# A two-layer hybrid encoder on one core: 512-column matmuls over high and low activations in the gate and up projections

## The chip, the cores and the metric

The kernel runs on one core of one Trainium2 chip. The time is the device time of one execution in microseconds, the median of several runs. A profile is one execution of the same program, recorded instruction by instruction. The engines in it are PE (the matmul engine, whose weight loads are listed as PEld), DVE (the vector engine), ACT (the scalar engine) and SP, which here only issues DMAs. POOL does nothing in this kernel.

## The reference

A sequence of 256 tokens of width 1024 goes through two layers. Each layer is a gated feed-forward sub-layer at half weight, a token-mixing sub-layer (retention, stick-breaking attention and a state-space mixer side by side) and a second feed-forward sub-layer. All is float32. Cut to what matters here:

```python
def swiglu(u, wg, wu, wd):
    return (jax.nn.silu(u @ wg) * (u @ wu)) @ wd

for l in range(DEPTH):                       # DEPTH = 2
    mod = (cond @ ada_w[l] + ada_b[l])       # shift, scale and gate of the sub-layers
    u = modulate(rmsnorm(h, norm_ffn1[l]), mod[0], mod[1])
    h = h + 0.5 * (1.0 + mod[2]) * swiglu(u, ffn1_wg[l], ffn1_wu[l], ffn1_wd[l])
    ...                                      # token mixing
    u = modulate(rmsnorm(h, norm_ffn2[l]), mod[6], mod[7])
    h = h + 0.5 * (1.0 + mod[8]) * swiglu(u, ffn2_wg[l], ffn2_wu[l], ffn2_wd[l])
```

The width of the feed-forward layer is 2816, which is 11 blocks of 256 columns.

## The kernel before

**Products in three parts.** PE multiplies in a rounded float32 form (`fp32r`). To keep float32 accuracy the kernel splits every weight and every activation into a high part, rounded to that form, and a low part, the rest. A product is then three matmuls that add up in one place of PSUM: high weights times high activations, high weights times low activations, low weights times high activations (`mm3`). Each matmul has 128 x 128 weights and 256 columns, the 256 tokens. Each matmul instruction has its own weight load in the profile, also where two in a row use the same weights.

**Units.** The weights come as units of 1 MB: one gate block (g), one up block (u) or one down block (d) of 256 columns or rows. A unit has two halves. For each half ACT copies the raw weights into the high part (`hi`, L306) and DVE subtracts to get the low part (`lo`, L307). There are eight buffers each for `hi` and `lo`. `half` and `need` see to it that, when PE's code comes to a half, the splits of the seven halves behind it have been issued ahead of it. A split whose buffer is still in use waits for PE. The order in which units are fetched and split is a fixed list (`SEQ`). Between the weight units it also holds 80 units of the modulation weights `ada_w`, two DVE instructions each (`raw_a`, L266); where they fall is set by the table `ADA_SPANS`. They are densest in the two feed-forward sub-layers of the first layer.

**A feed-forward sub-layer** (`ffn`) goes through the blocks j. For each j PE runs the gate projection into one PSUM bank (`pg`), then the up projection into another (`pu`), and then a down unit of an earlier block (`dn`). ACT takes the silu straight from `pg` (L195, called in `ffn`), DVE multiplies by `pu` straight from PSUM (L611), and `gated` splits the product into high and low (ACT and DVE, 512 columns each). The down unit of block j runs only after the gate and up units of block j+1. All engines take their instructions in the order in which the code issues them.

**PSUM.** There are eight banks of 512 float32 columns. A ring of four one-bank tiles serves `pg`, `pu`, the lead and the mixing sub-layer; four more banks hold the output sums (`dn`).

**The lead.** In all sub-layers but the first, the first gate and up units (four blocks of 128 columns, f = 0 to 3) run on activations that are not yet normalised (`hgh`, `hgl`), so that PE works while the norm is computed (`lead`). They go into four banks `ld`, 258 columns each. At the end, for each f, PE finishes the last two of eight steps, ACT reads one column (`lbias`), and DVE scales the rest (`lt`, L483). Between these, DVE and ACT make the normalised activations (`nt`, `uh`, `ul`). The next two units run interleaved step by step (`proj2`), since the activations only just become ready. The first sub-layer uses `start` for its first three blocks instead.

**Counts.** 76 gate and up units run outside leads and start: 8 blocks in the first feed-forward sub-layer and 10 in each of the other three, two units each. A unit has 8 steps over the width and 2 column blocks, so 16 products of three matmuls: 1216 in all.

Of the kernel before, what the change touches and what calls it, by code (L numbers as in the profile page):

```python
# [155 lines left out]
class Trunk:  # L156
# [5 lines left out]
    def __init__(self, ctx, tc, io):  # L162
        self.tc, self.nc, self.io = tc, tc.nc, io
        pool = lambda name, bufs, **kw: ctx.enter_context(tc.tile_pool(name=name, bufs=bufs, **kw))
        self.cp = pool("const", 1)
        self.rawp = pool("raw", self.NRAW)
        self.hip = pool("whi", self.NHALF)
        self.lop = pool("wlo", self.NHALF)
        self.t2 = pool("t2", 5)
        self.sm = pool("small", 2)  # L170
        self.ring = pool("ringp", 4, space=PSUM)
        self.pool = pool
        self.early = tc.tile_pool(name="early", bufs=self.NEARLY)
        self.earlyp = self.early.__enter__()
        self.raw = {}
        self.w = {}
        self.sent = 0
        self.done = 0
        self.ready = -1
        self.procs = []  # L180
        self.table = None
# [18 lines left out]
    def mm3(self, out, w, u, start, flip=False):  # L200
        for n, (a, b) in enumerate(((0, 0), (0, 1), (1, 0))):
            x, y = (u[b], w[a]) if flip else (w[a], u[b])
            self.mm(out, x, y, start and n == 0)

    def bank(self, name):
        return self.ring.tile([P, 512], F32, tag="ring", name=name)

    def open_acc(self, pairs):
        self.accs = self.tc.tile_pool(name="accp", bufs=2 if pairs else 4, space=PSUM)
# [99 lines left out]
    def setup(self):  # L309
        nc, io = self.nc, self.io  # L310
        self.params = self.cp.tile([P, NPAR], F32, name="params")
        self.consts = self.cp.tile([P, NCST], F32, name="consts")
        self.cond = self.cp.tile([P, 1024], F32, name="cond")
        self.wdt = self.cp.tile([P, L, 8, 8], F32, name="wdt")
        self.mods = self.cp.tile([P, NA * 2], F32, name="mods")
        self.h = self.cp.tile([P, KD, S], F32, name="h")
        self.uh = self.cp.tile([P, KD, S], FR, name="uh")
        self.ul = self.cp.tile([P, KD, S], FR, name="ul")
        self.rs = self.cp.tile([P, S], F32, name="rs")
        self.mats = self.cp.tile([P, 4, P], FR, name="mats")  # L320
        self.eps = self.cp.tile([P, 1], F32, name="eps")
        nc.vector.memset(self.eps, EPS)
        nc.sync.dma_start(out=self.cond, in_=io["c"].broadcast_to([P, 1024]))
        nc.sync.dma_start(out=self.params, in_=io["params"])
        for _ in range(self.NRAW + self.NEARLY + 1):
            self.send()
        self.silu(out=self.cond, in_=self.cond)
# [121 lines left out]
        self.nc.vector.scalar_tensor_tensor(out=self.ul[:, c], in0=t, scalar=self.mods[:, self.shift + c:self.shift + c + 1],  # L449
                                            in1=self.uh[:, c].bitcast(F32), op0=ALU.add, op1=ALU.subtract)  # L450

    def lead(self, n, ends):
        nc = self.nc
        banks = [self.bank("ld") for _ in range(4)]

        def go(k, f):
            hf = k // 4
            hi, lo = self.w[n + f // 2, hf]
            cs = slice((f % 2) * P, (f % 2) * P + P)
            gh, gl = self.hg[hf]  # L460
            self.mm3(banks[f][:, 0:258], [hi[:, k % 4, cs], lo[:, k % 4, cs]], (gh[:, k % 4], gl[:, k % 4]), k == 0)

        self.need(n + 1, 1, 2)
        for k in range(6):
            if k == 5:
                self.norm_sum(self.acc("nps"))
                self.need(n + 1, 1, 3)
                self.norm_rstd()
                self.need(n + 1, 1, 4)
            for f in range(4):  # L470
                go(k, f)
        self.norm_bcast()
        bias = self.sm.tile([P, 4], F32, tag="lbias", name="lbias")
        ts, us = [], []
        for f in range(4):
            for k in (6, 7):
                go(k, f)
            nc.scalar.activation(out=bias[:, f:f + 1], in_=banks[f][:, 256:257], func=AF.Copy)
            us.append(self.apply_a(f))
            if f % 2 == 0:  # L480
                t = self.tk2("lt")
            ts.append(t[:, (f % 2) * 256:(f % 2) * 256 + 256])
            nc.vector.tensor_tensor(out=ts[f], in0=banks[f][:, 0:256], in1=self.rs, op=ALU.mult)  # L483
# [55 lines left out]
    def proj_k(self, bank, w, k, flip, banks):  # L539
        w = [t[:, k % 4] for t in w]  # L540
        for f in range(2):
            if flip:
                self.mm3(banks[f], w, [t[:, f * P:(f + 1) * P] for t in self.u(k)], k == 0, True)
            else:
                cs = slice(f * P, (f + 1) * P)
                self.mm3(bank[:, f * 256:(f + 1) * 256], [t[:, cs] for t in w], self.u(k), k == 0 and f == 0)

    def proj(self, bank, n, flip=False, banks=None):
# [14 lines left out]

    def ffn(self, w0, gate_col, prep, start=None):
        nc = self.nc
        self.open_acc(False)
        n = w0 + 2
        pend = []

        def gated(sg):  # L570
            g = self.tk4("g", FR)
            gh, gl = (g[:, 2 * i:2 * i + 2] for i in range(2))
            flat = lambda t: t.rearrange("p a b -> p (a b)")
            self.split(flat(gh), flat(gl), sg)
            pend.append([(gh[:, f], gl[:, f]) for f in range(2)])

        def ends(f, t, b):
            v = sg[:, (f % 2) * 256:(f % 2) * 256 + 256]
            if f < 2:
                self.silu(out=v, in_=t, bias=b)  # L580
            else:
                nc.vector.scalar_tensor_tensor(out=v, in0=t, scalar=b, in1=v, op0=ALU.add, op1=ALU.mult)

        g0 = 1
        if start:
            g0 = GS
            banks = start()
            n = w0 + 2 * GS
            self.need(n, 0, 2)
            for j in range(GS):  # L590
# [3 lines left out]
                gated(sg)  # L594
        else:
            sg = self.tk2("sg")
            self.lead(w0, ends)
            gated(sg)
        accs = None
        for j in range(g0, NJ):  # L600
            pg, pu = self.bank("pg"), self.bank("pu")
            pair = j == 1
            if pair:
                self.proj2(n, (pg, False, None), (pu, False, None))
            else:
                self.proj(pg, n)
            sg = self.tk2("sg")
            self.silu(out=sg, in_=pg)
            if not pair:
                self.proj(pu, n + 1)  # L610
            nc.vector.tensor_tensor(out=sg, in0=sg, in1=pu, op=ALU.mult)  # L611
# [12 lines left out]
        self.out_unit(accs, n, pend.pop(0), False, True, gate)  # L624
        self.close_acc()

    def mix(self, l, w0, gate_col, prep):
        nc = self.nc
        st = {}
        flat = lambda t: t.rearrange("p a b -> p (a b)")  # L630
        V = lambda t, n: flat(t).rearrange("p (a b) -> p a b", a=n)
        self.open_acc(True)
        dt = self.sm.tile([P, 2, 8], F32, tag="dt", name="dt")
        dta = self.sm.tile([P, 2, 8], F32, tag="dta", name="dta")
# [316 lines left out]
        for o, kk in enumerate(W_OUT_ORDER):  # L951
# [5 lines left out]
            self.out_unit(accs, n, mov, o == 0, o == 5, gate)  # L957
            n += 1
        self.close_acc()

    def run(self):
        nc = self.nc
# [8 lines left out]
        for l in range(L):  # L971
            m, n = l * 72, l * NSUB
            self.ffn(n, m + 16, prep, None if l else lambda: self.start(*first))
            self.mix(l, n + NF, m + 40, prep)
            self.ffn(n + NF + NM, m + 64, prep)
        mean = self.bank("mean")[:, 0:256]
        for n, sq in enumerate(self.sq):
            for f in range(2):
# [9 lines left out]
        for b, o in enumerate(out):  # L988
            for f in range(2):
# [3 lines left out]
                else:  # L993
                    nc.scalar.activation(out=o[:, f], in_=o[:, f], func=AF.Identity, bias=sh)
            nc.sync.dma_start(out=self.io["out"][:, 2 * b:2 * b + 2], in_=o)


def _pack(inp):
# [96 lines left out]
```

## Time and profile before

| | |
|---|---|
| device time, median of 3 runs | 1162.9 us (1162.77 to 1163.27) |
| span of the profiled execution, first to last instruction | 1161.9 us |
| feed-forward sub-layers in the span, about | 27 to 219, 409 to 599, 599 to 789, 970 to 1150 us |
| mixing sub-layers, about | 219 to 409, 789 to 970 us |
| granted PE clock | 0.998 |
| weights and other data read | 280 MB |

The profiled execution's own device time is not listed apart from its span. The median of the runs is 1.0 us above the span: what lies around the first and the last instruction.

In a group's row stand line, engine, operation, names (out <- in), shapes and count, then the busy time of the group in us, the mean ns of one instruction, and the idle time of its engine just ahead of them with what ended it. In a timeline row stand the start in us, the duration, engine, line, names and shapes; idle time ahead of the row is in brackets. Matmuls overlap: one of 256 columns is listed with 280 ns, while the next starts 0.12 us after it, so what one costs is the distance of the starts. `f32` in a row of PE stands for both float32 forms.

### The profile page before, as it was taken

Reading aid. Unit: us, or ns where it says so; the run is one execution under the profiler, and the core shown is the slowest. Engines: PE = TensorE matmul, PEld = TensorE weight load, DVE = VectorE, ACT = ScalarE, POOL = GpSimd, SP = SyncE. Lnnn points to the kernel's source line nnn. Section 1 sums busy time; section 2 is a strip of 40 time slices with the busy share of each in tenths; the row PEclk is TensorE's granted clock in tenths of the full one; section 3 lists DMA queues with packets and bytes.
Section 4 is the critical chain, followed back from the end, with each engine's and each line's share of the span. In section 5 each row is a group of like instructions: output and inputs, shape, how many; then the busy total and the mean of one; then the engine's idle time right before and its main releaser. Section 6 shows DMA issues by size and latency. Waiting matters only on the chain.

```text
span 1161.9 us, 22045 instructions
## 1 busy us (share of the span) xinstructions
PE 1126.8 (97%) x9316; PEld 1115.7 (96%) x9316; DVE 893.3 (77%) x1300; ACT 619.0 (53%) x870; POOL 0.2 (0%) x4
## 2 busy tenths in 40 slices
PE   1999999999999999999999999999999999999996
PEld 1999999999999999999999999999999999999996
DVE  6988786788778788898488788667886877977544
ACT  4464434586874464444466444457687546544432
POOL 0000000000000000000000000000000000000000
PEclk9999999999999999999999999999999999999999
DMA  9879898357454539999536988643655452987610
GB/s 376 338 265 366 320 361 333 129 214 276 163 190 155 182 142 370 347 372 359 188 110 258 345 322 307 254 182 144 256 182 186 177 189 80 351 331 283 235 58 37
DMA packets 39555, 282.63 MB, mean 243 GB/s; under 512 B 4384, under 2 KB 4640, under 8 KB 5408
## 3 DMA queue, kind: packets, MB, share of 16 engines
q1 hardware_dynamic: 39456, 281.22, 64.6%
q8 instruction: 73, 1.20, 0.4%
q14 instruction: 26, 0.21, 0.1%
HBM read 280.15 MB, written 1.05 MB: 242 GB/s over the span
## 4 chain that ended last, share of the span: by engine, by line
PE 96%; DVE 2%; ACT 1%; DMA 1%; issue 0%; SPq 0%; ACTq 0%; DVEq 0%
PE dn L198 21%; PE pu L198 19%; PE pg L198 19%; PE pj L198 14%; PE ld L198 7%; PE wo L198 6%; PE pv L198 4%; DVE raw_a L266 1%; PE seg L198 1%; PE nps L198 1%; DMA h<-in_x 1%; PE tail L198 1%; PE sz L198 1%; PE rn L198 1%; PE yb L198 1%; PE rs L198 0%
## 5 line engine op out<-in xcount | busy, mean ns | idle before, releaser
L307 DVE TENSOR_TENSOR lo<-raw_w,hi 128x1024 fp32r<-128x1024 f32 x368 | 441.6, 1222 | 152.8 <-ACT hi L306 152.5
L306 ACT ACTIVATE hi<-raw_w 128x1024 fp32r<-128x1024 f32 x368 | 380.3, 1053 | 252.4 <-DMA raw_w<-in_w 118.1
L198 PE MATMUL dn<-g,hi 128*128 128x256 f32 x1408 | 250.7, 280 | 0.0
L198 PEld LDWEIGHTS dn<-g,hi 128*128 128x128 f32 x1408 | 215.7, 189 | 0.0
L266 DVE CUSTOM_DVE_ANT_0 raw_a<-raw_a,cond,params 128x1024 f32<-128x1024 f32 x160 | 198.8, 1280 | 0.3 <-DMA raw_a<-in_ada 0.3
L198 PE MATMUL dn<-g,lo 128*128 128x256 f32 x704 | 197.3, 280 | 0.0
L198 PE MATMUL pu<-uh,hi 128*128 128x256 f32 x608 | 171.2, 282 | 0.0
L198 PE MATMUL pu<-ul,hi 128*128 128x256 f32 x608 | 171.2, 282 | 0.0
L198 PE MATMUL pg<-ul,hi 128*128 128x256 f32 x608 | 171.1, 281 | 0.0
L198 PE MATMUL pg<-uh,hi 128*128 128x256 f32 x608 | 171.1, 281 | 0.0
L198 PE MATMUL pg<-uh,lo 128*128 128x256 f32 x608 | 170.9, 281 | 0.0
L198 PE MATMUL pu<-uh,lo 128*128 128x256 f32 x608 | 170.8, 281 | 0.0
L198 PEld LDWEIGHTS dn<-g,lo 128*128 128x128 f32 x704 | 132.8, 189 | 0.0
L198 PE MATMUL pj<-uh,hi 128*128 128x256 f32 x448 | 127.9, 285 | 0.0
L198 PE MATMUL pj<-ul,hi 128*128 128x256 f32 x448 | 126.0, 281 | 0.0
L198 PE MATMUL pj<-uh,lo 128*128 128x256 f32 x448 | 125.9, 281 | 0.0
L198 PEld LDWEIGHTS pu<-uh,lo 128*128 128x128 f32 x608 | 114.9, 189 | 0.0
L198 PEld LDWEIGHTS pg<-uh,lo 128*128 128x128 f32 x608 | 114.8, 189 | 0.0
L198 PEld LDWEIGHTS pu<-ul,hi 128*128 128x128 f32 x608 | 114.5, 188 | 0.0
L198 PEld LDWEIGHTS pg<-ul,hi 128*128 128x128 f32 x608 | 114.4, 188 | 0.0
L198 PEld LDWEIGHTS pg<-uh,hi 128*128 128x128 f32 x608 | 114.4, 188 | 0.0
L198 PEld LDWEIGHTS pu<-uh,hi 128*128 128x128 f32 x608 | 114.3, 188 | 0.0
(189 smaller groups left out, 1791.2 us busy)
## 6 DMA issues: line engine op xcount, KB each, us to landing
raw_w<-in_w SPq DMA_DIRECT2D x184, 1024.0 KB, 5.8
raw_a<-in_ada SPq DMA_DIRECT2D x80, 1024.0 KB, 6.5
consts<-in_consts SPq DMA_DIRECT2D x1, 1216.0 KB, 10.1
h<-in_x SPq DMA_DIRECT2D x1, 1024.0 KB, 7.0
out<-fin SPq DMA_DIRECT2D x4, 256.0 KB, 2.3
cond<-in_c SPq DMA_DIRECT2D x1, 512.0 KB, 4.3
mats<-in_mats SPq DMA_DIRECT2D x1, 256.0 KB, 7.1
params<-in_params SPq DMA_DIRECT2D x1, 176.0 KB, 4.4
```

The source lines that it names most:

```text
L198: self.nc.tensor.matmul(out, lhsT=lhsT, rhs=rhs, start=start, stop=True, skip_group_check=True)
L266: nc.vector.tensor_tensor_reduce(out=raw[:, f * 1024:(f + 1) * 1024], in0=raw[:, f * 1024:(f + 1) * 1024], in1=self.cond, scale=1.0, scala ...
L306: self.nc.scalar.activation(out=hi, in_=src, func=AF.Copy)
L307: self.nc.vector.tensor_tensor(out=lo, in0=src, in1=hi.bitcast(F32), op=ALU.subtract)
```

## The change

High and low activations now lie side by side in one tile (`us`). For the 76 gate and up units, one matmul takes the high weights against both, 512 columns, into a full bank: columns 0 to 255 get the high part, 256 to 511 the low part. A second matmul of 256 columns adds low weights times high activations onto the first half. A block of 256 weight columns thus needs two banks (`bank2`), and the ring has two such tiles in place of four of one bank. The sum of the two halves is made at reading (`fold`): ACT copies the low half from PSUM into SBUF, DVE adds the high half from PSUM. The silu then works on SBUF, and the up projection is folded too before the multiplication. The leads of the three later feed-forward sub-layers take their four banks as two of the two-bank tiles. The ring is opened and closed in each sub-layer. Leads, down units, the mixing sub-layer and the order of the weights keep their matmuls.

```diff
+    def lead_banks(self, pairs):
+        if pairs:
+            return [t[:, f] for t in [self.bank2("ld") for _ in range(2)] for f in range(2)]
+        return [self.bank("ld") for _ in range(4)]
...
+    def wide_k(self, bank, w, k):
+        hi, lo = (t[:, k % 4] for t in w)
+        both = self.us[:, k].rearrange("p a b -> p (a b)")
+        for f in range(2):
+            cs = slice(f * P, (f + 1) * P)
+            self.mm(bank[:, f], hi[:, cs], both, k == 0)
+            self.mm(bank[:, f, 0:256], lo[:, cs], self.uh[:, k], False)
...
+    def wide2(self, n, names):
+        banks = [self.bank2(name) for name in names]
+        for k in range(KD):
+            if k % 4 == 0:
+                wa = self.half(n, k // 4, 1)
+                wb = self.half(n + 1, k // 4, 3)
+            self.wide_k(banks[0], wa, k)
+            self.wide_k(banks[1], wb, k)
+        return banks
+
+    def fold(self, bank, name):
+        t = self.tk2(name)
+        v = t.rearrange("p (a b) -> p a b", a=2)
+        self.nc.scalar.activation(out=v, in_=bank[:, :, 256:512], func=AF.Copy)
+        self.nc.vector.tensor_tensor(out=v, in0=v, in1=bank[:, :, 0:256], op=ALU.add)
+        return t
...
         for j in range(g0, NJ):
-            pg, pu = self.bank("pg"), self.bank("pu")
             pair = j == 1
             if pair:
-                self.proj2(n, (pg, False, None), (pu, False, None))
+                pg, pu = self.wide2(n, ("pg", "pu"))
             else:
-                self.proj(pg, n)
-            sg = self.tk2("sg")
-            self.silu(out=sg, in_=pg)
+                pg = self.wide("pg", n)
+            sg = self.fold(pg, "sg")
+            self.silu(out=sg, in_=sg)
             if not pair:
-                self.proj(pu, n + 1)
-            nc.vector.tensor_tensor(out=sg, in0=sg, in1=pu, op=ALU.mult)
+                pu = self.wide("pu", n + 1)
+            t = self.fold(pu, "su")
+            nc.vector.tensor_tensor(out=sg, in0=sg, in1=t, op=ALU.mult)
             gated(sg)
```

What moves in the instruction order is shown at three places. Names carry buffer numbers; `lo68_0` is the low part of the first half of unit 68, and a wait names the engine whose semaphore is waited for. In the second feed-forward sub-layer of the first layer unit 67 is the gate unit of block 3, 68 its up unit, 69 the down unit behind them.

DVE, in the order before, around the up unit of block 2 (`raw_a` is the modulation work):

```order
L307 TENSOR_TENSOR lo68_0_4936<-raw_w68_4422,hi68_0_4935 128x1024 [waits DMAHW5_49,PE_49,Activation_49]
L307 TENSOR_TENSOR lo68_1_4966<-raw_w68_4422,hi68_1_4965 128x1024 [waits PE_49,Activation_49]
L266 ISA raw_a35_4601,mods_85<-raw_a35_4601,cond_83,params_81 128x1024 [waits DMAHW6_49,DVE_49]
...
L307 TENSOR_TENSOR lo69_0_5000<-raw_w69_4749,hi69_0_4999 128x1024 [waits DMAHW7_49,PE_49,Activation_49]
L611 TENSOR_TENSOR sg_4963<-sg_4963,pu_4900 128x512 [waits PE_49]
L307 TENSOR_TENSOR g_5028<-sg_4963,g_5028 128x512 [waits Activation_49]
L307 TENSOR_TENSOR lo69_1_5032<-raw_w69_4749,hi69_1_5031 128x1024 [waits Activation_49]
```

DVE, the same place in the changed kernel:

```order
L321 TENSOR_TENSOR lo68_0_4697<-raw_w68_4217,hi68_0_4696 128x1024 [waits DMAHW5_49,PE_49,Activation_49]
L592 TENSOR_TENSOR sg_4716<-sg_4716,pg_4669 128x512 [waits Activation_49]
L321 TENSOR_TENSOR lo68_1_4722<-raw_w68_4217,hi68_1_4721 128x1024 [waits Activation_49]
L280 ISA raw_a35_4398,mods_82<-raw_a35_4398,cond_80,params_78 128x1024 [waits DMAHW6_49,DVE_49]
...
L321 TENSOR_TENSOR lo69_0_4748<-raw_w69_4530,hi69_0_4747 128x1024 [waits DMAHW7_49,PE_49,Activation_49]
L592 TENSOR_TENSOR su_4767<-su_4767,pu_4720 128x512 [waits Activation_49]
L663 TENSOR_TENSOR sg_4716<-sg_4716,su_4767 128x512 [waits DVE_49]
L321 TENSOR_TENSOR g_4771<-sg_4716,g_4771 128x512 [waits Activation_49]
L321 TENSOR_TENSOR lo69_1_4775<-raw_w69_4530,hi69_1_4774 128x1024 [waits Activation_49]
```

Two adds (L592) have come in: that of `pg` between the two splits of unit 68, that of `pu` ahead of the multiplication.

ACT at the same place, before:

```order
L306 ACTIVATE hi68_0_4935<-raw_w68_4422 128x1024 [waits DMAHW5_49,PE_49,Activation_49]
L195 ACTIVATE sg_4963<-pg_4899 128x512 [waits PE_49]
L306 ACTIVATE hi68_1_4965<-raw_w68_4422 128x1024 [waits DVE_49]
L306 ACTIVATE hi69_0_4999<-raw_w69_4749 128x1024 [waits DMAHW7_49,DVE_49,PE_49]
L306 ACTIVATE g_5028<-sg_4963 128x512 [waits DVE_49]
```

ACT, changed:

```order
L320 ACTIVATE hi68_0_4696<-raw_w68_4217 128x1024 [waits DMAHW5_49,PE_49,Activation_49]
L591 ACTIVATE sg_4716<-pg_4669 128x512 [waits PE_49]
L194 ACTIVATE sg_4716<-sg_4716 128x512 [waits DVE_49]
L320 ACTIVATE hi68_1_4721<-raw_w68_4217 128x1024 [waits Activation_49]
L320 ACTIVATE hi69_0_4747<-raw_w69_4530 128x1024 [waits DMAHW7_49,PE_49,Activation_49]
L591 ACTIVATE su_4767<-pu_4720 128x512 [waits PE_49]
L320 ACTIVATE g_4771<-sg_4716 128x512 [waits DVE_49]
```

The silu (L194) now stands behind a wait for DVE, and the split of `hi68_1` stands behind the silu.

PE at the end of the lead of the same sub-layer, changed: the last step of block f = 1 and of f = 3, and the first matmuls of the next two units.

```order
L197 MATMUL ld_4311<-hgh_4207,lo59_1_4118 128x258
L197 MATMUL ld_4311<-hgh_4207,hi59_1_4117 128x258 [waits DVE_49]
...
L197 MATMUL ld_4312<-hgh_4207,hi60_1_4145 128x258 [waits DVE_49]
...
L197 MATMUL pg_4488<-us_84,hi61_0_4175 128x512 [waits PE_49]
L197 MATMUL pg_4488<-us_84,lo61_0_4176 128x256
...
L197 MATMUL pu_4489<-us_84,hi62_0_4213 128x512 [waits DVE_49]
```

PE, before, from the last matmul of the lead on:

```order
L198 MATMUL ld_4515<-hgh_4412,lo60_1_4351 128x258
L198 MATMUL pg_4691<-uh_87,hi61_0_4380 128x256 [waits DVE_49,Activation_49]
L198 MATMUL pg_4691<-ul_88,hi61_0_4380 128x256 [waits DVE_49]
L198 MATMUL pg_4691<-uh_87,lo61_0_4381 128x256
...
L198 MATMUL pu_4692<-uh_87,hi62_0_4418 128x256 [waits Activation_49]
```

Blocks f = 0 and 1 now share one tile `ld`, and f = 2 and 3 another. The end of f = 1 waits for DVE's reading of f = 0, that of f = 3 for the reading of f = 2, and the first matmul of `pu` for the reading of f = 3; before, none of these waits was there. In steady state the first matmul of each `pg` and `pu` now waits for DVE, whose add has freed the tile.

More of the change, by code (lines that the diff above doesn't have):

```diff
@@ L170, in __init__ @@
         self.sm = pool("small", 2)
-        self.ring = pool("ringp", 4, space=PSUM)
         self.pool = pool
@@ L203, in mm3, with open_ring, close_ring, bank2 @@
             self.mm(out, x, y, start and n == 0)
+    def open_ring(self, pairs):
+        self.rings = self.tc.tile_pool(name="ringp", bufs=2 if pairs else 4, space=PSUM)
+        self.ring = self.rings.__enter__()
+    def close_ring(self):
+        self.rings.__exit__(None, None, None)
     def bank(self, name):
         return self.ring.tile([P, 512], F32, tag="ring", name=name)
+    def bank2(self, name):
+        return self.ring.tile([P, 2, 512], F32, tag="ring", name=name)
+    def lead_banks(self, pairs):
+        if pairs:
+            return [t[:, f] for t in [self.bank2("ld") for _ in range(2)] for f in range(2)]
+        return [self.bank("ld") for _ in range(4)]
     def open_acc(self, pairs):
@@ L316, in setup @@
         self.h = self.cp.tile([P, KD, S], F32, name="h")
-        self.uh = self.cp.tile([P, KD, S], FR, name="uh")
-        self.ul = self.cp.tile([P, KD, S], FR, name="ul")
+        self.us = self.cp.tile([P, KD, 2, S], FR, name="us")
+        self.uh, self.ul = self.us[:, :, 0], self.us[:, :, 1]
         self.rs = self.cp.tile([P, S], F32, name="rs")
@@ L450, in apply_b, with lead @@
                                             in1=self.uh[:, c].bitcast(F32), op0=ALU.add, op1=ALU.subtract)
-    def lead(self, n, ends):
+    def lead(self, n, ends, pairs=False):
         nc = self.nc
-        banks = [self.bank("ld") for _ in range(4)]
+        banks = self.lead_banks(pairs)
         def go(k, f):
@@ L546, in proj_k, with wide @@
                 self.mm3(bank[:, f * 256:(f + 1) * 256], [t[:, cs] for t in w], self.u(k), k == 0 and f == 0)
+    def wide_k(self, bank, w, k):
[5 more added lines that the diff above has]
+            self.mm(bank[:, f, 0:256], lo[:, cs], self.uh[:, k], False)
+    def wide(self, name, n):
+        bank = self.bank2(name)
+        for k in range(KD):
+            if k % 4 == 0:
+                w = self.half(n, k // 4)
+            self.wide_k(bank, w, k)
+        return bank
+    def wide2(self, n, names):
+        banks = [self.bank2(name) for name in names]
+        for k in range(KD):
+            if k % 4 == 0:
+                wa = self.half(n, k // 4, 1)
[9 more added lines that the diff above has]
+        return t
     def proj(self, bank, n, flip=False, banks=None):
@@ L565, in ffn @@
         nc = self.nc
+        self.open_ring(not start)
         self.open_acc(False)
@@ L594, in ffn @@
                 gated(sg)
+            self.close_acc()
+            self.close_ring()
+            self.open_ring(True)
+            self.open_acc(False)
         else:
             sg = self.tk2("sg")
-            self.lead(w0, ends)
+            self.lead(w0, ends, True)
             gated(sg)
@@ L625, in ffn @@
         self.close_acc()
+        self.close_ring()
     def mix(self, l, w0, gate_col, prep):
@@ L631, in mix @@
         V = lambda t, n: flat(t).rearrange("p (a b) -> p a b", a=n)
+        self.open_ring(False)
         self.open_acc(True)
@@ L959, in mix @@
         self.close_acc()
+        self.close_ring()
     def run(self):
@@ L975, in run @@
             self.ffn(n + NF + NM, m + 64, prep)
+        self.open_ring(False)
         mean = self.bank("mean")[:, 0:256]
@@ L995, in run @@
             nc.sync.dma_start(out=self.io["out"][:, 2 * b:2 * b + 2], in_=o)
+        self.close_ring()
 def _pack(inp):
```

## The prediction

> **What bounds the kernel now.** First the page's busy times and the chain of work that ended last:
>
> ```profile
> PE 1126.8 (97%) x9316; PEld 1115.7 (96%) x9316; DVE 893.3 (77%) x1300; ACT 619.0 (53%) x870; POOL 0.2 (0%) x4
> ...
> PE 96%; DVE 2%; ACT 1%; DMA 1%; issue 0%; SPq 0%; ACTq 0%; DVEq 0%
> ```
>
> PE sets the end: fewer or shorter matmuls shorten the kernel as long as nobody makes PE wait. So the second look goes to the room that DVE has, by sub-layer (us, busy time and instructions of PE, PEld, DVE and ACT, then clock, DMA share, GB/s):
>
> ```profile
> 27.00:219.00 192.00, 191.17 (x1587) 190.88 (x1588) 157.73 (x203) 91.14 (x109) 0.00 (x0) 1.00 0.85 320
> ...
> 409.00:599.00 190.00, 189.69 (x1596) 189.39 (x1595) 153.78 (x212) 92.41 (x120) 0.00 (x0) 1.00 0.75 283
> 599.00:789.00 190.00, 189.84 (x1595) 189.59 (x1596) 144.34 (x196) 93.90 (x122) 0.00 (x0) 1.00 0.70 261
> ...
> 970.00:1150.00 180.00, 179.76 (x1514) 179.55 (x1514) 120.27 (x153) 80.84 (x99) 0.00 (x0) 1.00 0.57 211
> ```
>
> In the first layer's two feed-forward sub-layers DVE is busy 82% and 81% of the time, in the last one 67%. The change adds to DVE just there.
>
> **The matmuls.** A gate unit of 48 matmuls (timeline of PE; the first of `pg` and of the `pu` behind it):
>
> ```profile
> 498.18 0.28 PE L198 MATMUL pg<-uh,hi 128*128 128x256 f32 x1
> ...
> 503.90 0.28 PE L198 MATMUL pu<-uh,hi 128*128 128x256 f32 x1
> ```
>
> 5.72 us / 48 = 119 ns for one of 256 columns with its weight load. The change turns 1216 pairs, 238 ns each, into one of 512. How long that takes, no row shows. Near it stand one of 384 columns in the same form (`seg`) and two of the plain float32 form:
>
> ```profile
> 299.37 0.40 PE L198 MATMUL seg<-segm,mats 128*128 128x384 f32 x2
> ```
>
> ```profile
> L198 PE MATMUL seg<-segm,mats x64: 221/280/423, 299.4 to 894.3; 128*128 128x384 f32 x32, 128*128 128x128 f32 x32
> ```
>
> ```profile
> L198 PE MATMUL tail<-sbe,mats 128*128 128x384 f32 x16 | 6.5, 486 | 0.0
> ...
> L198 PE MATMUL rn<-diag,mats 128*128 128x512 f32 x8 | 4.1, 591 | 0.0
> ```
>
> The first row holds one of 384 and one of 128 columns; the second lasts 0.22 (the 221 of the second row), so it started 0.18 us after the first. From 256 to 384 columns, 119 became about 178: in a straight line 512 take 237, no gain. From the other side: `rn` against `tail` gives 105 ns for 128 further plain columns, 0.82 ns each. If that form runs each column twice (my reading), a turn is 0.41 ns, 256 columns take 105 and 14 of the 119 belong to the change of weights; paid once, 512 take 210 + 14 = 224, a gain of 14. At 384 some 20 are left over, so the truth lies between. I take 229, **9 ns per pair: 1216 x 9 = 10.9 us less**, 0.144 us per unit (16 pairs), with 0 and 17 us as ends.
>
> **The lead.** In three sub-layers its four banks become two tiles, and three waits arise. Rows of PE and DVE in the third feed-forward sub-layer, in order of time:
>
> ```profile
> 600.23 0.28 PE L198 MATMUL ld<-hgh,hi 128*128 128x258 f32 x1
> ...
> 600.63 0.42 DVE L483 TENSOR_TENSOR lt<-ld,rs 128x256 f32<-128x256 f32 x1
> ...
> 601.36 0.42 DVE L483 TENSOR_TENSOR lt<-ld,rs 128x256 f32<-128x256 f32 x1
> ...
> 601.67 0.28 PE L198 MATMUL ld<-hgh,hi 128*128 128x258 f32 x1
> ...
> 602.38 0.28 PE L198 MATMUL pg<-uh,hi 128*128 128x256 f32 x1
> ...
> 602.49 0.42 DVE L483 TENSOR_TENSOR lt<-ld,rs 128x256 f32<-128x256 f32 x1
> ...
> 603.61 0.41 DVE L483 TENSOR_TENSOR lt<-ld,rs 128x256 f32<-128x256 f32 x1
> ```
>
> Block f = 1 (six matmuls from 600.23) must now wait for the first `lt`, to 601.05 and a handover of some 0.05: it starts at 601.1, its last result is there 0.59 + 0.29 later, at 601.98. The second `lt` so starts at 602.0 in place of 601.36; the third keeps its distance (1.13) and ends at 603.55. Block f = 3 waits for it: 603.6 in place of 601.67, **1.9 us late**, and so does `pg`. The fourth `lt` then ends near 604.9; `pu`, 0.7 behind `pg`, comes at 605.0 and loses nothing more. Nothing stands between f = 3 and `pg` on PE that could hide it: 3 x 1.9 = **5.8 us more**. DVE's own chain is 0.9 late behind the lead. As lower end only the wait of `pu` counts (some 1.0 each, 3 us); as upper end a handover of 0.2 at each of three waits (7 us).
>
> **The folds.** Each of the 76 units gets an ACT copy and a DVE add, and the silu goes through DVE. The nearest rows, also 128x512 from PSUM, and the splits:
>
> ```profile
> L306 ACT ACTIVATE hi<-raw_w 128x1024 fp32r<-128x1024 f32 x368 | 380.3, 1053 | 252.4 <-DMA raw_w<-in_w 118.1 <-PE dn L198 43.5 <-PE pg L198 28.1
> ...
> L195 ACT ACTIVATE sg<-pg 128x512 f32<-128x512 f32 x38 | 22.5, 591 | 41.4 <-PE pg L198 41.4
> ```
>
> ```profile
> L611 DVE TENSOR_TENSOR sg<-sg,pu 128x512 f32<-128x512 f32 x38 | 26.0, 683 | 16.8 <-PE pu L198 16.8
> ```
>
> ACT gets 76 x 0.59 = 45 us on 619 of 1162 and has room. DVE gets 0.68 per add, 0.60 as back-to-back instructions overlap by 0.08. The add of `pg` costs more: the next instruction of DVE is a `lo` whose `hi` stands on ACT behind the silu, and the silu waits for the add. So DVE stands idle for 0.59 + 1.05 + handover = 1.7 us. A block j costs DVE 2 x 0.6 + 1.7 = **2.9 us more**, idle or busy, while PE's part of a block gets 0.29 shorter. Where DVE has no room, PE then waits for the add that frees its tile: the `pg` of block j+1 needs the add of the `pg` of block j, which stands on DVE behind splits seven halves ahead of PE.
>
> *Second feed-forward sub-layer.* DVE's groups from 445.3 to 542.1 us, that is from the place of block 2's add of `pg` to that of block 8's:
>
> ```profile
> L307 DVE TENSOR_TENSOR lo<-raw_w,hi 128x1024 fp32r<-128x1024 f32 x36 | 43.0, 1222 | 6.0 <-ACT hi L306 6.0
> L266 DVE CUSTOM_DVE_ANT_0 raw_a<-raw_a,cond,params 128x1024 f32<-128x1024 f32 x30 | 37.3, 1280 | 0.3 <-DMA raw_a<-in_ada 0.3
> L307 DVE TENSOR_TENSOR g<-sg,g 128x512 fp32r<-128x512 f32 x6 | 4.2, 693 | 4.2 <-ACT g L306 4.2
> ```
>
> In these 97 us DVE idles 6.0 us for `hi`, and 4.2 in handovers that stay. Its place at the end, and PE's first matmul of the next `pg`:
>
> ```profile
> 540.81 1.23 DVE L307 TENSOR_TENSOR lo<-raw_w,hi 128x1024 fp32r<-128x1024 f32 x1 [0.35 <-ACT hi L306]
> ```
>
> ```profile
> 549.35 0.28 PE L198 MATMUL pg<-uh,hi 128*128 128x256 f32 x1
> ```
>
> DVE is there 7.3 us ahead of PE (542.04 to 549.35). And right behind the lead:
>
> ```profile
> 425.77 0.68 DVE L611 TENSOR_TENSOR sg<-sg,pu 128x512 f32<-128x512 f32 x1
> 427.15 0.69 DVE L307 TENSOR_TENSOR g<-sg,g 128x512 fp32r<-128x512 f32 x1 [0.70 <-ACT g L306]
> 428.10 3.50 DVE L307 TENSOR_TENSOR lo<-raw_w,hi 128x1024 fp32r<-128x1024 f32 x3 [0.26 <-ACT hi L306]
> ```
>
> There add, silu, copy and add now follow one another ahead of the multiplication (0.65 + 0.6 + 0.6 + 0.65): 2.6 us, with the lead's 0.9 makes 3.5. DVE comes later by 3.5 + 6 x 2.9 + 0.65 (the add itself), less the 6.0 of idle time that it can use: 15.5. PE comes 16 x 0.144 = 2.3 earlier, less 1.9 from the lead. **PE waits 15.5 + 0.4 - 7.3 = 8.6, with some rest of the DMA waits 9 us**; if none of the 6.0 is used 14.6, if the 1.7 hides wholly, none.
>
> *First feed-forward sub-layer.* The same from block 3 to 8 (74.5 to 170.8 us):
>
> ```profile
> L307 DVE TENSOR_TENSOR lo<-raw_w,hi 128x1024 fp32r<-128x1024 f32 x34 | 41.1, 1223 | 9.9 <-ACT hi L306 9.8
> ```
>
> ```profile
> 169.43 1.23 DVE L307 TENSOR_TENSOR lo<-raw_w,hi 128x1024 fp32r<-128x1024 f32 x1 [1.26 <-ACT hi L306]
> ```
>
> ```profile
> 178.74 0.28 PE L198 MATMUL pg<-uh,hi 128*128 128x256 f32 x1
> ```
>
> 5 x 2.9 + 0.65 - 9.9 + 1.7 against 8.1: -1.1 with all idle time used, 8.8 with none. I take **1 us**, as DMA is at 0.85 over the whole sub-layer. The third sub-layer's DVE idles 9 us more than the second's, the last one's far more: nothing there.
>
> **Sum.** -10.9 + 5.8 + 9 + 1 = +4.9. Against the profiled execution: 1161.9 + 4.9 = 1166.8 of span; the median lies 1.0 above the span, so **1167.8 us**, 0.4% slower.
>
> **Rivals.** (1) *A 512-column matmul pays only its columns*, 215 ns, near twice 105 plus a few. Gain 23 x 1216 = 28 us, 0.37 per unit. But DVE paces the second sub-layer: PE is earlier there by 16 x 0.226 = 3.6 more and waits 12.6; in the first by 12 x 0.226 = 2.7 more, 3.7. 1162.9 - 28 + 5.8 + 12.6 + 3.7 = **1157**, faster than before. It decides once a pair costs under some 223. For it: plain float32 leaves next to nothing above its columns. Against it: the 384 row. The Trainium skill ("TensorE: Matmul & The Clock Gate", Back-to-back issue gap) states this rule, N / 2.4 + 2.5 ns at full clock, 215.8 for 512. By it 256 columns would take 109; the trace has 119, so the rule does not hold as it stands for this form.
>
> (2) *DVE finds the room*: the wait behind the silu hides, or the adds cost little, and PE never waits in steady state: 1162.9 - 10.9 + 5.8 + 1 = **1159**, faster. For it: DVE idles 6.0 and 9.9 us in the dense stretches. Against it: the order puts silu and `hi` behind the add without anything for DVE in between.
>
> (3) *512 columns cost as two times 256* (the straight line): 1162.9 + 5.8 + 6.7 = **1175**.
>
> **Chances.** Forecast 0.50 (1162 to 1173), rival 1 0.15, rival 2 0.15, rival 3 0.13; 0.07 for others, among them a DVE that recovers nothing (1181). The range reaches from rival 1 to rival 3: 1156 to 1176. A measurement of this kernel tells 0.2% (2.3 us) from no change. Faster than 1160.6: 0.15 + 0.11 + 0.04 of the forecast's lower end = 0.30. Within: 0.22. Slower: 0.48.
>
> **What would show it.** The first `pg` and `pu` of consecutive units: 16 x (512 + 256) in 5.57 us says 229 for the wide one, 5.35 rival 1, 5.7 rival 3. `pg` behind the three leads: 1.9 us of idle PE with DVE's `lt` as releaser. Idle PE ahead of `pg` and `pu` near 446 to 560 us in the second feed-forward sub-layer, released by DVE's add (L592), some 9 us in all, and next to none in the third and last. On DVE a `lo` behind each add of `pg` with 1.7 us of waiting for `hi`. If PE's idle time lies elsewhere, or DVE in that stretch is idle as before, the account of the folds is wrong; if PE runs without gaps and the time is still above 1163, the price of the wide matmul is.

## The result, and the profile after

The changed kernel takes **1176.9 us** (median of 4 runs, 1175.6 to 1178.3) against 1163.1 us for the kernel before in the same session: a ratio of 1.0121, 95% interval 1.0107 to 1.0135. It is slower, as forecast, but by 13.8 us instead of 4.9, and lies 0.9 us above the end of the range. The profiled execution has a span of 1174.2 us, 12.3 more than before. One of the ten executions of the kernel of e2 below took 6304 us; it is left out of that kernel's ratio.

The page's busy times and the chain of work that ended last:

```profile
PE 1124.9 (96%) x8100; PEld 1054.0 (90%) x8100; DVE 938.5 (80%) x1376; ACT 651.9 (56%) x946; POOL 0.2 (0%) x4
...
PE 77%; DVE 14%; ACT 3%; issue 3%; DMA 3%; SPq 0%; DVEq 0%; ACTq 0%
```

PE has 1216 instructions less, and DVE now holds 14% of the chain, up from 2%. Where PE waited (waits of PE; tile, releaser and line, then us in total, number of waits and longest):

```profile
PE ld L197 <- DVE lt L497: 5.5, 6, 1.1
PE pu L197 <- DVE su L592: 4.5, 4, 1.1
PE pg L197 <- DVE sg L592: 3.5, 4, 0.9
...
PE dn L197 <- DVE g L321: 0.3, 1, 0.3
...
PE ld L197 <- DVE hgl L435: 0.2, 1, 0.2
```

None of the five is there in the kernel before. The first three are the two new kinds of wait that the prediction names: the leads, and the adds that free a tile. The two short ones stand at the end of the first feed-forward sub-layer (213 and 219 us). By stage (us, busy time and instructions of PE, PEld, DVE, ACT; the first and the second feed-forward sub-layer):

```profile
27.00:219.00 192.00, 189.74 (x1329) 177.23 (x1329) 165.11 (x215) 95.75 (x122) 0.00 (x0) 1.00 0.82 316
409.00:609.00 200.00, 191.09 (x1279) 173.50 (x1277) 166.04 (x233) 102.28 (x141) 0.00 (x0) 1.00 0.71 268
```

The second has become 10 us longer. The rows of its lead and of the next one give it exactly (groups of the tile `ld` of the kernel before, with the time of the first start):

```profile
L198 PE MATMUL ld<-hgh,hi x2: 281/284/286, 399.4 to 399.7; 128*128 128x258 f32 x2
L198 PE MATMUL ld<-hgh,hi x26: 278/283/469, 589.1 to 599.9; 128*128 128x258 f32 x26
```

and of the changed kernel:

```profile
L197 PE MATMUL ld<-hgh,hi x1: 280/280/280, 399.8 to 399.8; 128*128 128x258 f32 x1
L197 PE MATMUL ld<-hgh,hi x3: 278/280/283, 599.3 to 600.0; 128*128 128x258 f32 x3
```

From lead to lead 189.7 us became 199.5: 9.8 of the 12.3 are lost in this one sub-layer.

**One wide matmul.** Two units of the third feed-forward sub-layer, where PE waits only in the lead (timeline of PE: first `pg`, first `pu`, first `dn` behind it):

```profile
699.87 0.40 PE L197 MATMUL pg<-us,hi 128*128 128x512 f32 x1
...
705.49 0.39 PE L197 MATMUL pu<-us,hi 128*128 128x512 f32 x1
...
711.11 0.39 PE L197 MATMUL dn<-g,hi 128*128 128x256 f32 x2
```

A unit takes 5.62 us, not the 5.57 of the forecast: 351.3 ns per product of a wide and a narrow matmul. The narrow one keeps 118 ns (mean distance of starts), so the wide one costs **233 ns**, and a product gains 5.9 ns, not 9.

**One wait.** The first `pg` behind the down unit in the second feed-forward sub-layer (timeline of PE):

```profile
449.22 0.28 PE L197 MATMUL dn<-g,lo 128*128 128x256 f32 x1
450.32 0.50 PE L197 MATMUL pg<-us,hi 128*128 128x512 f32 x1 [0.82 <-DVE sg L592]
450.66 0.28 PE L197 MATMUL pg<-us,lo 128*128 128x256 f32 x1
```

and the add that it waits for, with what DVE does behind it (timeline of DVE):

```profile
449.59 0.68 DVE L592 TENSOR_TENSOR sg<-sg,pg 128x512 f32<-128x512 f32 x1
451.92 1.23 DVE L321 TENSOR_TENSOR lo<-raw_w,hi 128x1024 fp32r<-128x1024 f32 x1 [1.65 <-ACT hi L320]
453.06 1.28 DVE L280 CUSTOM_DVE_ANT_0 raw_a<-raw_a,cond,params 128x1024 f32<-128x1024 f32 x1
```

The start after the add's end is what DVE sets; and DVE then stands 1.65 us, since the `hi` of its next split is queued on ACT behind the silu. The listed wait of 0.82 understates the loss. From start to start there are 1.10 us where 0.12 would do, and 0.34 behind the first wide matmul where 0.23 is usual: 1.09 in all, 0.27 more than listed.

### The profile page after: what moved, and what is told of

Read it like the earlier page. It is cut to its first block, busy times and chain, and to the rows that moved or that the text cites. A ratio compares the mean times of both kernels' runs of the same rounds, so it can differ in the third digit from the quotient of the medians.

```text
span 1174.2 us, 19703 instructions
## 1 busy us (share of the span) xinstructions
PE 1124.9 (96%) x8100; PEld 1054.0 (90%) x8100; DVE 938.5 (80%) x1376; ACT 651.9 (56%) x946; POOL 0.2 (0%) x4
## 4 chain that ended last, share of the span: by engine, by line
PE 77%; DVE 14%; ACT 3%; issue 3%; DMA 3%; SPq 0%; DVEq 0%; ACTq 0%
PE dn L197 15%; PE pj L197 14%; PE pg L197 13%; PE pu L197 12%; PE ld L197 7%; PE wo L197 6%; DVE raw_a L280 5%; DVE lo L321 5%; PE pv L197 4%; DMA raw_w<-in_w 2%; ACT hi L320 2%; PE seg L197 1%; DVE sg L663 1%; PE nps L197 1%; PE tail L197 1%
## 5 line engine op out<-in xcount | busy, mean ns | idle before, releaser
L197 PE MATMUL pu<-us,hi 128*128 128x512 f32 x608 | 217.2, 396 | 4.6 <-DVE su L592 4.5
L197 PE MATMUL pg<-us,hi 128*128 128x512 f32 x608 | 216.6, 396 | 3.5 <-DVE sg L592 3.5
L197 PEld LDWEIGHTS dn<-g,hi 128*128 128x128 f32 x1408 | 215.8, 189 | 2.2 <-DVE g L321 0.5
L197 PE MATMUL pu<-us,lo 128*128 128x256 f32 x608 | 170.3, 280 | 0.0
L197 PE MATMUL pg<-us,lo 128*128 128x256 f32 x608 | 170.2, 280 | 0.0
L197 PE MATMUL pj<-us,hi 128*128 128x256 f32 x896 | 163.7, 283 | 0.0
L197 PEld LDWEIGHTS pg<-us,hi 128*128 128x128 f32 x608 | 114.1, 188 | 30.0 <-DVE sg L592 4.3
L197 PEld LDWEIGHTS pj<-us,hi 128*128 128x128 f32 x896 | 137.5, 188 | 0.7 <-issue 0.7
L197 PE MATMUL pj<-us,lo 128*128 128x256 f32 x448 | 125.9, 281 | 0.0
L197 PEld LDWEIGHTS pg<-us,lo 128*128 128x128 f32 x608 | 114.5, 188 | 0.0
L197 PEld LDWEIGHTS pu<-us,lo 128*128 128x128 f32 x608 | 114.3, 188 | 0.0
L194 ACT ACTIVATE sg<-sg 128x512 f32<-128x512 f32 x38 | 24.1, 633 | 95.7 <-DVE sg L592 95.7
```

Of the source, the lines that this page charges most:

```text
L194: self.nc.scalar.activation(func=AF.Silu, **kw)
L197: self.nc.tensor.matmul(out, lhsT=lhsT, rhs=rhs, start=start, stop=True, skip_group_check=True)
```

## Experiments

My theory after the result: the time comes from three separate places, (a) the wide matmul gains less than forecast, (b) the leads wait for `lt`, (c) PE waits for the adds because the silu stands ahead of a split on ACT. A rival for (c) is that DVE merely has too much to do, wherever the silu stands; for (a), that the price of 512 columns belongs to this order or these banks. The first four kernels ran beside a kernel before of 1162.6 us (19 runs), the next four beside 1162.5 (14 runs), the last two beside 1162.8 (7 runs). The change itself ran beside 1163.1, so a difference between it and one of these kernels carries some 0.5 us of difference between the sessions.

**e1: the lead over separate tiles.** Blocks 0 and 1 in a two-bank tile each, 2 and 3 in banks of the output sums.

```diff
-            return [t[:, f] for t in [self.bank2("ld") for _ in range(2)] for f in range(2)]
+            return [self.bank2("ld")[:, 0] for _ in range(2)] + [self.acc("ld") for _ in range(2)]
```

> The changed kernel, but each of the lead's four blocks lies in a tile of its own (two of them in the free banks of the output sums), so that no block shares a tile with another. Theory (tile sharing makes the three waits): PE's waits for `lt` in the three leads go (6.8 us with what the weight loads show), `pg` stands 13.3 us behind the lead's start as before the change, not 15.6; the second feed-forward sub-layer gives back some 1.3 us of it, since DVE paces it: 1171 us. Rival (the lead is late because of two-bank tiles or the new pools as such): the leads stay at 15.6 us and the time at 1176.5.

Measured 1174.5 us, ratio to the kernel before 1.0101 (1.0086 to 1.0116): 2.4 us less than the change, a miss. Waits of PE:

```profile
PE ld L197 <- DVE h L534: 4.3, 3, 1.6
```

The `lt` waits are gone, but the banks of the output sums are still being read into `h` (L534) when the next lead wants them. The edit exchanged one wait for another, and the waits for the adds are as long as before (8.1 us listed). It leaves (b) open rather than refuting it.

**e2: the silu later.** The silu of `pg` is issued behind the up unit, so the split stands ahead of it on ACT.

```diff
             sg = self.fold(pg, "sg")
-            self.silu(out=sg, in_=sg)
             if not pair:
                 pu = self.wide("pu", n + 1)
+                self.silu(out=sg, in_=sg)
             t = self.fold(pu, "su")
+            if pair:
+                self.silu(out=sg, in_=sg)
```

> The changed kernel, but the silu of `pg` is issued on ACT behind the splits of the up unit, not ahead of them; no work is added or taken away. Theory (what paces DVE is above all its wait of 1.7 us for a `hi` that stands behind the silu): the waits of PE for the adds (some 10.5 us in the first two feed-forward sub-layers) shrink to under 2 us: 1167 us. Rival (the adds themselves, 0.6 us twice per block, fill DVE): at most 2 to 3 us are won, 1174 us, and DVE's waits for `hi` are as before.

Measured 1164.5 us, ratio 1.0016 (1.0006 to 1.0025): **12.4 us less than the change**, more than expected. The profiled spans differ by 11.9: 10.2 are the waits for the adds, 0.8 the two short waits at the end of the first sub-layer, and some 0.7 lies ahead of PE's first matmul, which comes at 11.4 to 12.2 us in the different runs. No wait for L592 is left in PE's list of waits, and the chain is PE's again:

```profile
PE 95%; DVE 3%; ACT 1%; DMA 1%; issue 0%; SPq 0%; ACTq 0%; DVEq 0%
```

DVE's group of splits from 445.3 to 546 us, in the changed kernel

```profile
L321 DVE TENSOR_TENSOR lo<-raw_w,hi 128x1024 fp32r<-128x1024 f32 x34 | 40.9, 1222 | 11.6 <-ACT hi L320 11.6
```

and in e2:

```profile
L321 DVE TENSOR_TENSOR lo<-raw_w,hi 128x1024 fp32r<-128x1024 f32 x37 | 44.4, 1222 | 2.5 <-ACT hi L320 2.4
```

The adds are all still there (76 of them, as before the edit), and DVE as a whole is no less busy (940.5 us against 938.5). What has gone is 9 us of DVE standing for `hi`, in the stretch in which PE waited. So (c) is not the adds' own time, but the order on ACT.

**e3: both edits.**

> Both edits at once. Theory: what is left is the gain of the matmuls, 1216 x 5.9 ns = 7.2 us, less some 1 to 3 us of waits: 1157 to 1159 us, faster than before the change. Rival (waits move elsewhere: DVE or DMA pace the second sub-layer all the same): 1163 us or more.

Measured 1162.2 us, ratio 0.9995 (0.9986 to 1.0005), no difference from the kernel before and short of the 1157 to 1159 expected. The lead part again gives 2.3 of its 7 us: the waits for `h` are there as in e1 (4.3 us listed), and one wait for the add of `pg` came back (1.0).

**e4: two matmuls in place of the wide one**, all else as in the change.

```diff
-            self.mm(bank[:, f], hi[:, cs], both, k == 0)
+            self.mm(bank[:, f, 0:256], hi[:, cs], self.uh[:, k], k == 0)
+            self.mm(bank[:, f, 256:512], hi[:, cs], self.ul[:, k], False)
```

> The changed kernel, tiles and folds alike, but each 512-column matmul is again two of 256 columns into the two halves of the bank. Theory (a 512-column matmul takes 233 ns, two narrow ones 238, and the one behind them 1 ns more): some 1216 x 5.9 ns = 7.2 us more on PE, less 1 to 2 us where DVE paces: 1182 us. Rival (the wide matmul gains nothing, the spacing changed for another reason, as the addresses of the tiles): 1176.5 us, and the spacing within `pg` stays at 351 ns per product.

Measured 1180.4 us, ratio 1.0155 (1.0137 to 1.0173): 3.5 us more than the change. The mean distance of starts is 120 ns, 119 before the change. In the traces the gate and up units so take 8.5 us more, and 2.9 of it is taken back, as PE waits less for the adds when it comes later (5.7 us listed for L593, the same add, in place of 8.0); the spans differ by 4.9, the medians by 3.5.

**e7: the same edit on top of e2**, where no add is waited for.

> The silus late (as in e2_silu_late), with two matmuls of 256 columns into the two halves of the bank in place of the one of 512. This measures the wide matmul where DVE paces nothing. My account: 1216 x 5.9 ns = 7.2 us more than e2_silu_late, 1171.7, since no wait takes part of it up (in e4_narrow it cost only 3.5, as PE there waited for DVE anyway). Rival, that a wide matmul gains what e4_narrow showed, 3 ns each: 1168. Rival 3 of the prediction, that it gains nothing: 1164.5.

Measured 1172.1 us, ratio 1.0079 (1.0066 to 1.0093): 7.6 us more than e2. In the traces the gate and up units take 7.3 us more, 6.0 ns per product. One wait for the add of `pg` (0.8 listed) came back, and some 0.5 us less lies elsewhere in the span. The wide matmul is a gain, of the size that the distances of starts gave (5.9 ns), and where DVE paces PE a part of it does not arrive.

**e8: less for DVE in the second feed-forward sub-layer**, silu as in the change. Six modulation units move from there into the mixing sub-layer ahead of it.

```diff
-ADA_SPANS = (((17, 11, 30), (7, 8, 28), (18, 6, 28)), ((14, 10, 29), (6, 10, 28), (10, 6, 25)))
+ADA_SPANS = (((17, 11, 30), (13, 8, 28), (12, 6, 28)), ((14, 10, 29), (6, 10, 28), (10, 6, 25)))
```

> The changed kernel with six of the modulation units of the first layer moved from the second feed-forward sub-layer (18 there before, 12 now) to the mixing sub-layer ahead of it (13 in place of 7); two DVE instructions of 1.28 us each per unit, 15 us of DVE work less in the second sub-layer. Everything else as in the change, the silu early. Theory, that the 9.3 us of waiting for L592 there come of DVE having too little room in that stretch: they fall to 0 to 1, and 1176.5 becomes about 1168 (the mixing sub-layer has room on DVE; if it has not, up to 1172). Rival, that the chain of copy, add, silu and split costs PE its time by its length, whatever else DVE does: 1176.

Measured 1171.9 us, ratio 1.0081 (1.0067 to 1.0095), 5.0 less than the change. The second feed-forward sub-layer, from 405 to 595 us here:

```profile
405.00:595.00 190.00, 187.98 (x1273) 172.65 (x1272) 150.85 (x206) 99.91 (x139) 0.00 (x0) 1.00 0.65 248
```

and PE's waits in this kernel that were not in the change's list, with what is left for L592:

```profile
PE rs L197 <- DVE rq L903: 1.4, 1, 1.4
PE pu L197 <- DVE su L592: 1.1, 1, 1.1
PE seg L197 <- DVE sbm L877: 0.8, 1, 0.8
PE tail L197 <- DVE sbe L870: 0.7, 1, 0.7
PE rn L197 <- DVE diag L355: 0.6, 1, 0.6
...
PE yb L197 <- DVE segE L807: 0.5, 1, 0.5
```

All seven waits of the second sub-layer are gone with the silu early, and the sub-layer lasts 190 us instead of 199.5. The one that is left is in the first sub-layer, which this edit does not touch. The mixing sub-layer had no room for the six units: it ends at 405 instead of 400 us, with the other five waits above. DVE still stands 11.4 us for `hi` between 445.3 and 546 us, as in the change (11.6), but PE no longer waits for it. So both are needed for (c): a DVE with little room, and 1.65 us of it standing idle per block. Either remedy removes the wait.

**e6: lead blocks dealt alternately over the two tiles**, with e2.

```diff
-            return [t[:, f] for t in [self.bank2("ld") for _ in range(2)] for f in range(2)]
+            ts = [self.bank2("ld") for _ in range(2)]
+            return [ts[f % 2][:, f // 2] for f in range(4)]
```

> The silus late (as in e2_silu_late), and the four lead blocks dealt over the two tiles alternately: f = 0 and 2 share one, 1 and 3 the other. No bank is added. My account: PE waits for the reading of a block only when it comes back to the same tile, so the wait of f = 1 goes and those of f = 2, f = 3, pg and pu are short (some 0.15, 0, 0.4 and 0.4 us by the distances of the readings); a lead costs 1.05 us more than before the change in place of 2.35: 1164.5 - 3.9 = 1160.6. Rival, that the lead is late because of the handovers as such and not their order: 1164.5.

Measured 1159.5 us, ratio 0.9977 (0.9967 to 0.9987): 5.0 us less than e2. No bank is added and no arithmetic changed; only the block that shares a tile comes two later instead of one. Of 5.5 us listed for `lt` there remains:

```profile
PE pu L197 <- DVE lt L498: 0.3, 2, 0.2
```

By the distances of starts a lead still costs 1.1 us more than before the change, as expected.

**e5: the lead and the pair behind it as before the change**, with e2: four one-bank tiles, three 256-column matmuls per product, silu and multiplication straight from PSUM; the two-bank tiles are opened only behind that pair.

```diff
-        self.open_ring(not start)
+        self.open_ring(False)
...
-            self.lead(w0, ends, True)
+            self.lead(w0, ends)
...
-                pg, pu = self.wide2(n, ("pg", "pu"))
+                pg, pu = self.bank("pg"), self.bank("pu")
+                self.proj2(n, (pg, False, None), (pu, False, None))
+                sg = self.tk2("sg")
+                self.silu(out=sg, in_=pg)
+                t = pu
...
             gated(sg)
+            if pair:
+                self.close_acc()
+                self.close_ring()
+                self.open_ring(True)
+                self.open_acc(False)
```

> The silus of the up unit's stretch issued late (as in e2_silu_late), and the lead with the pair of units behind it as before the change: four one-bank tiles, the two units interleaved in three matmuls of 256 columns each, silu and multiplication straight from PSUM; the two-bank tiles are opened only behind that pair, three times in all. My account: the three leads fall from 15.65 back to 13.3 us from their start to the first pg (7.1 us), six units lose the gain of the wide matmul (6 x 16 x 5.9 ns = 0.6 us), so 1164.5 - 7.1 + 0.6 = 1158, about 0.4% faster than the kernel before, which is the 7.2 us of the matmuls less a rest of some 2. Rival, that the waits come back where the pools change (as they did in e1_lead_apart, as waits for readers of other banks): the first pg behind the pair waits 1 to 2 us in each of three sub-layers, 1161 to 1164.

Measured **1156.1 us** (1155.95 to 1156.74), ratio 0.9945 (0.9933 to 0.9958): faster than both kernels, by 0.55% than the one before. The 8.5 us against e2 are more than the 6.5 expected: besides the 2.4 us per lead, the first `pu` behind the lead no longer waits (0.3 us each). The six narrow units cost their 0.6 us (357 ns per product in place of 351). Some 0.5 us of the difference lies ahead of the first lead, where both kernels do the same: runs differ by that. Reopening the tiles costs no wait; PE's list ends with what it had before the change:

```profile
PE nps L197 <- DVE sq L439: 11.7, 1, 11.7
PE ld L197 <- ACT hi L320: 10.3, 1, 10.3
PE nps L197 <- DVE diag L355: 2.2, 4, 1.7
PE ld L197 <- DVE lo L321: 0.5, 1, 0.5
PE mean L197 <- DVE sq L439: 0.2, 1, 0.2
```

What is left of the change is the matmuls: 70 units x 16 x 5.9 ns = 6.6 us, against 6.4 measured.

**e9: the wide matmul at 384 columns** in seven of eight steps, on e5. It leaves out the low activations of the last 128 tokens there.

```diff
-            self.mm(bank[:, f], hi[:, cs], both, k == 0)
+            n = 384 if k else 512
+            self.mm(bank[:, f, 0:n], hi[:, cs], both[:, 0:n], k == 0)
```

> e5_lead_old, with the wide matmul of steps 1 to 7 cut to 384 columns (step 0 keeps 512, so that the whole bank is written). Left out: low activations of the last 128 tokens in seven of eight steps of the gate and up units. Measured is the distance of starts of one of 384 columns. If columns cost evenly, it lies on the line through 119 (256 columns) and 233 (512): 176 ns, a fixed part of some 4.7 ns and 0.446 ns per column. If the price of 512 has a surcharge of its own (the reading that 512 could have cost 224 to 229 but for it), 384 comes out nearer to 170. The time itself is no evidence, since shorter matmuls let DVE pace more of PE: 1100 to 1130.

One run, 1112.8 us. Timeline of PE, the first and the eighth of a row of products:

```profile
723.78 0.34 PE L197 MATMUL pg<-us,hi 128*128 128x384 f32 x1
723.96 0.28 PE L197 MATMUL pg<-us,lo 128*128 128x256 f32 x1
...
725.83 0.34 PE L197 MATMUL pg<-us,hi 128*128 128x384 f32 x1
```

2.05 us / 7 = 293 ns per product, less 118 for the narrow one: 175. The mean over all 974 undisturbed ones is 175.8, where the line through 119 and 233 has 176. The price is a straight line; 512 columns have no surcharge of their own.

**e10: the order wide, wide, narrow, narrow**, on e5.

```diff
             self.mm(bank[:, f], hi[:, cs], both, k == 0)
+        for f in range(2):
+            cs = slice(f * P, (f + 1) * P)
             self.mm(bank[:, f, 0:256], lo[:, cs], self.uh[:, k], False)
```

> e5_lead_old with the four matmuls of a step in another order: the wide ones of both column blocks, then the two narrow ones, in place of wide, narrow, wide, narrow. Same matmuls, same banks. Theory, that a wide matmul costs its columns whoever stands behind it: start to start 233 and 118 as before, 1156. Rival, that part of the price is the change between wide and narrow or between the banks of one tile: the wide one followed by a wide one costs 4 to 9 ns less or more, 2 to 5 us in the time.

Measured 1158.0 us, ratio 0.9958 (0.9942 to 0.9975). A wide one costs 234 ns ahead of a wide one and 232 ahead of a narrow one; neither is 4 ns from 233, so the price does not come from the neighbour. Whether the 1.9 us against e5 are real is open, since the intervals overlap; it is in any case no gain. In the traces 1.2 us of it lie in the gate and up units, where a narrow one ahead of a wide one costs 120 ns and not 118, and 0.5 ahead of PE's first matmul.

## Why the prediction was wrong in size

The sign, the places and the order of the effects were right; three sizes were too favourable, all to the same side: the gain of the wide matmul, the price of a lead, and what the sum put at nothing.

| term | forecast, us | measured, us |
|---|---|---|
| 1216 wide matmuls | -10.9 | -7.2 (1216 x 5.9 ns) |
| three leads | +5.8 | +8.0 (3 x 2.38, and 3 x 0.3 at `pu`) |
| second feed-forward sub-layer | +9 | +8.8 (6.9 listed, and 7 x 0.27) |
| first feed-forward sub-layer | +1 | +1.4 (1.1 listed, and 0.27) |
| rest | 0 | +1.3, of which 0.8 in two waits of PE for `g` and `hgl` at the end of the first sub-layer; the other 0.5 is not traced |
| sum, span | +4.9 | +12.3 |
| outside the span | +1.0 | 1.7 |

The 1.0 of the last row was a misreading of the numbers before. In every run whose time and span are both known, the time lies 1.7 to 1.9 us above the span. The 1.0 was the distance between a median and the span of an execution that by this took some 1163.6 us itself, 0.5 above the median of 1163.1. The changed kernel's profiled execution took 1175.9, 1.0 below its median. That is how 12.3 between the spans and 13.8 between the medians go together.

**The matmuls** are the step that failed most: 229 was taken, 233 is true, 3.7 us. The row of 384 columns stood in the prediction and said 237 in a straight line, 4 too many. Against it I set a reading of the plain float32 form: "If that form runs each column twice (my reading), a turn is 0.41 ns", and 14 of the 119 ns for the change of weights. That gave 224, 9 too few, and 229 was taken between the two. e9 and e10 show no such part: with 119, 175.8 and 233 the form costs 0.446 ns per column and only 4.7 ns per instruction. That is why joining two matmuls gains 5.9 ns (4.7, and 1 ns that the narrow one behind it gains) and not 9 or 14. The row in the same form was worth more than the argument from another one. And the plain rows themselves do not leave 14 above their columns (timeline of PE, kernel before):

```profile
371.92 1.02 PE L198 MATMUL rn<-diag,mats 128*128 128x512 f32 x2
372.77 0.28 PE L198 MATMUL rn<-mats,rsq 128*128 128x1 f32 x2
```

Two of 512 columns take 0.85 us from start to start, 425 ns each; at the prediction's 0.82 ns per column 420 are columns, and 5 are left. The 14 came from putting the plain form's price per column (0.41 ns a turn) under the rounded form, whose own is 0.446.

The Trainium skill's rule ("TensorE: Matmul & The Clock Gate", Back-to-back issue gap, N / 2.4 + 2.5 ns), which that section gives as the gap of isolated matmuls and which rival 1 names, gives 162.5 and 215.8 for 384 and 512 columns. The measured 175.8 and 233 decide against it for this form, as the 119 for 256 had already.

**The leads** were 1.9 us each by the prediction's chain and became 2.38. The third sub-layer's lead in the changed kernel (timeline of PE, ACT and DVE):

```profile
611.29 0.39 PE L197 MATMUL ld<-hgh,hi 128*128 128x258 f32 x1 [0.72 <-DVE lt L497]
...
612.32 0.17 ACT L492 ACTIVATE lbias<-ld 128x1 f32<-128x1 f32 x1 [0.97 <-PE ld L197]
...
612.52 0.42 DVE L497 TENSOR_TENSOR lt<-ld,rs 128x256 f32<-128x256 f32 x1 [0.89 <-ACT lbias L492]
...
613.65 0.42 DVE L497 TENSOR_TENSOR lt<-ld,rs 128x256 f32<-128x256 f32 x1
...
614.12 0.39 PE L197 MATMUL ld<-hgh,hi 128*128 128x258 f32 x1 [1.13 <-DVE lt L497]
...
614.95 0.40 PE L197 MATMUL pg<-us,hi 128*128 128x512 f32 x1
```

Block f = 1 starts 12.0 us behind the lead's start (599.3), 0.9 late as forecast, and the third `lt` keeps its distance of 1.13 from the second, as forecast. But from f = 1 to the second `lt` there are 1.23 us, where the prediction had 0.90: ACT's reading of one column (`lbias`), which the prediction's chain left out, lies between the matmul and DVE, with its handovers 0.25, and behind a wait PE's next matmul comes 0.1 later. With the same 0.1 behind the wait of f = 3, 1.9 becomes 2.35. The prediction then let `pu` lose nothing; it lost 0.3 each time.

**The second feed-forward sub-layer**: 9 forecast, 8.8 found, in seven waits from 450 to 559 us, with the 1.65 us (forecast: 1.7) of DVE standing behind each add of `pg`. This was the hardest term and the best one; e2 and e8 show its mechanism from both sides. That the size came out so close is in part luck. With the measured gain of the wide matmul (1.5 us earlier in place of 2.3) and the measured lead (2.7 late in place of 1.9) the same sum gives 15.5 - 1.2 - 7.3 = 7.0. The errors cancel against DVE's idle time: the sum let DVE use all 6.0 us of it, while DVE still stood 11.6 us for `hi` there, 1.7 more than six times 1.65. Third and last sub-layer: no wait for L592, as forecast. In the first, 1.4 for 1.

**The rivals.** That DVE finds the room (rival 2) did not happen in the change, but e2 shows what it needs: the silu behind the split. Rival 3 came nearest in time, but not by its reason: 233 lies about halfway between its 238 and the forecast's 229. Its time, 1175, took the leads and the second sub-layer at the forecast's sizes. The range ended there, although the leads' own upper end (7 us) and the 14.6 of the second sub-layer pointed the same way. Rival 3 with the leads at 7 in place of 5.8 would have been 1176.6, and a spread of one or two us between runs comes on top. The range was built from the cases one at a time, and not from two of them together.

## What to carry to other kernels

Before joining two matmuls, take the price of the larger one from a row of the same number form, and expect only the fixed part of an instruction as the gain: here 4.7 of 119 ns. A sum that is moved from PSUM accumulation to DVE cost little by itself here (e5); look at what the order of ACT's queue puts between that add and DVE's next instruction, and move that first (e2: some 12 us by moving one call). Where two blocks come to share one tile, let them be two that do not follow one another in time (e6), and keep the old layout where the stretch is short and its waits are on the path (e5).

## What I had not expected of the hardware

- The rounded float32 form costs an even 0.446 ns per column from 256 to 512 columns at a granted clock of 0.996 to 0.998, with 4.7 ns fixed, each instruction with its own weight load: 119, 175.8 and 233 ns.
- A wait of PE for an add or for `lt` cost 0.27 us more here than the trace lists: the listed idle time starts at the end of the last matmul (0.28 long, when the next would start after 0.12), and the first one behind the wait is followed 0.1 late.
- An output bank handed to another use made the lead wait 1.4 us for the last reader of that bank (e1), where the waits that it was to replace were 1.8 us listed.
